# Hybrid diffusion step on one core: channel-mixer spills issued by GpSimd, modulation sums four steps behind, no modulation steps where the down product begins

## The chip, the cores and the metric

One core of a Trainium2 chip runs the whole step in one launch. The metric is the device time of that launch in microseconds. Engines are named as in the profile: PE (matrix products; PEld its weight loads), DVE (vector), ACT (scalar activations), POOL (GpSimd), SP (the queue that issues nearly all DMAs). All arithmetic is float32: a product of two float32 matrices is made of three matmuls, with each operand split into a rounded high part and the low rest.

## What is computed

Two layers over 1024 latent and 256 prompt tokens of width 1024. What matters here is the SwiGLU channel mixer that closes each layer, and the modulation vectors that scale, shift and gate every sub-layer:

```python
def swiglu(h, w_gate_up, w_down):
    gu = h @ w_gate_up
    return (jax.nn.silu(gu[..., :FFN_HIDDEN]) * gu[..., FFN_HIDDEN:]) @ w_down
for l in range(DEPTH):
    mod_p = jax.nn.silu(c_ctx) @ w_mod[l] + b_mod[l]
    mod_s = (jax.nn.silu(c) @ w_mod[l] + b_mod[l])[:, None, :]
    sh1_p, sc1_p, g1_p, sh2_p, sc2_p, g2_p = jnp.split(mod_p, 6, axis=-1)
    ...
    xp = xp + g2_p * swiglu(hp, w_gate_up[l], w_down[l])
    xs = xs + g2_s * swiglu(hs, w_gate_up[l], w_down[l])
```

`w_mod[l]` is 1024 x 6144, `w_gate_up[l]` 1024 x 5632, `w_down[l]` 2816 x 1024. In layer 0 a parallel mixer (windowed attention beside multi-scale pooling) comes before, in layer 1 grouped-query attention.

## The kernel before

Tokens stand in three tiles `ti`: 0 and 1 are 512 latent tokens each, 2 is the prompt's 256. The order on each engine is the order in which the code is written (`manual_schedule`), and an engine that waits holds back all that is written behind it on that engine. SP too is such a queue.

**The gate-up loop** (`ffn`, from L864). The hidden width is 22 chunks `i` of 128 (`NHC`). The two latent tiles are multiplied by a Strassen-like scheme: per chunk `front` (L913) and `back` (L999) make seven products of 12 matmuls each (`prod`, L879), named by their right operand Q11, Q21, T2, T1, T3, Q22, T4, and DVE, ACT and POOL add them up (in `back`, POOL does L1018 and L1019). The prompt tile has two plain products (`dense`, `prompt_gate` and `up_prompt`). Chunks 0 and 1 run interleaved in `begin` (L958); the others are the rounds 2 to 21. Each product fills one of eight PSUM buffers (`psd`), which is free again when DVE or ACT has read it.

**Weights.** Each round needs four weight units, G, A, B and U: G and U are halves of `w_gate_up` as loaded, A and B are sums of them. `Weights.make` (L261) builds A with L271 and L272, B with L274 and L275, on POOL from the 15th unit on; then ACT rounds the unit (L280) and DVE makes its low rest (L282). There are four unit buffers, and `W.done` makes the next unit as soon as one is used up, so a unit is built about a round before PE needs it. Raw weights come by SP (L251).

**Spills.** The finished hidden activations are split (`hi_lo`: ACT L767, DVE L768) into a staging tile and written to device memory: per round two of 512 KB through the one buffer `x2_1` (`spill`, L892, its DMA L900: first tile 1, from `c12`, then tile 0, from `c21`) and one of 256 KB (`up_prompt`, L938, its DMA L945). All three are issued by SP.

**Modulation.** While PE works on the gate-up loop, DVE makes the next modulation vectors (`Mod`, L357). A job is 512 columns: eight accumulate steps (two instructions each, L386 or L388, on one 256 KB tile that SP loads, L318, two tiles ahead), then two empty steps, then two sums (`sum`, L397: PE transposes the accumulator, L400, DVE reduces it, L401), then `mod_done`: 13 steps. `mstep` (L875) takes one step; it stands at six places of a round: after Q11 (here F1), after T2, T1, T3, Q22 and T4 (B1 to B5). Layer 0's mixer carries 12 jobs, layer 1's two. Other jobs run in the input projection of layer 0 (four) and its output projection (two).

**Down.** `down(q)` (L1038) multiplies six groups of chunks (`GROUPS`, 2 or 4 chunks) by `w_down`: 24 products per group (`mix`, L1058), each added to the residual by DVE (L1067). The activations come back by SP (`load_h`, L902) and so does the residual (`load_x`, L908). In groups 0 to 4 `mix` takes a modulation step after every product of tile 0.

Of the kernel before, what the change touches and what calls it, by code (L numbers as in the profile page):

```python
# [9 lines left out]
F32 = mybir.dt.float32  # L10
# [15 lines left out]
NHC = HID // 128  # L26
# [97 lines left out]
def hybrid_step(ctx: ExitStack, tc: tile.TileContext, I: dict, O: list):  # L124
    nc = tc.nc
    pe, act, dve, pool, sp = nc.tensor, nc.scalar, nc.vector, nc.gpsimd, nc.sync
# [65 lines left out]
    class Background:  # L192
# [12 lines left out]
        def step(self, n=1, now=1 << 30):  # L205
            for _ in range(n):
                if not self.q or self.q[0][1] > now or self.q.pop(0)[2]():
                    return
# [102 lines left out]
    def dense(ps, w, A, ti):  # L311
        for k in range(8):
            dense_k(ps, w, A, ti, k)
# [7 lines left out]
    def mod_done(l, j, v):  # L321

        o = modv[:, l, 4 * j:4 * j + 4, :]
        dve.tensor_tensor(o, v, bmod[:, l, 4 * j:4 * j + 4, None].to_broadcast([128, 4, 2]), op=OP.add)
        six, half = j // 2, j % 2
        if six in (1, 4):
            k = six // 4
            g = norms[:, 2 * l + k, 4 * half:4 * half + 4, None].to_broadcast([128, 4, 2])
            dve.scalar_tensor_tensor(moda[:, l, k, 4 * half:4 * half + 4, :], o, 1.0, g, op0=OP.add, op1=OP.mult)
# [27 lines left out]
    class Mod:  # L357
# [14 lines left out]
        def step(self):  # L372
            if self.pending:
                f = self.pending.pop(0)
                if f:
                    f()
                return True
            if self.pos >= len(self.tiles):
                return False
            l, j, k = self.tiles[self.pos]  # L380
            t = self.loaded.pop(self.pos)[:, 0]
            if k == 0:
                self.acc = [(self.sums or npool).tile([128, 512], F32, name="nacc", bufs=2) for _ in range(2)]
            for c, a in enumerate(self.acc):
                if k == 0:
                    dve.tensor_scalar(a, t, cond_raw[:, k, c:c + 1], 0.0, op0=OP.mult, op1=OP.add)  # L386
                else:
                    dve.scalar_tensor_tensor(a, t, cond_raw[:, k, c:c + 1], a, op0=OP.mult, op1=OP.add)  # L388
            self.pos += 1
            self.load(self.pos + self.bufs)  # L390
            if k == 7:
                acc, v = self.acc, npool.tile([128, 32], F32, name="mv", bufs=2)[:, 0:8].rearrange("p (b x) -> p b x", x=2)
                self.pending = [None, None, lambda: self.sum(acc[0], v, 0), lambda: self.sum(acc[1], v, 1),
                                lambda: mod_done(l, j, v)]
            return True

# [10 lines left out]
    def mvec(l, six, k, c):  # L407
        return modv[:, l, 8 * six + k, c:c + 1]
# [357 lines left out]
    def hi_lo(hi, lo, src):  # L766
        act.activation(hi, src, AF.Copy)  # L767
        dve.tensor_tensor(lo, src, hi.bitcast(F32), op=OP.subtract)  # L768
# [95 lines left out]
    def ffn(W, l, x, A, g2, tail, md, xr):  # L864
# [8 lines left out]
        H, now = {}, [0]  # L873

        def mstep():  # L875
            if md is not None and now[0] > 1:
                md.step()

        def prod(w, off, name):  # L879
            pt = ps_tile()  # L880
            t = quad[name]
            for c in range(4):
                wh, wl = w[:, 0, off + 128 * c:off + 128 * c + 128], w[:, 1, off + 128 * c:off + 128 * c + 128]
                pe.matmul(pt, wh, t(0, c), start=(c == 0), stop=False)  # L884
                pe.matmul(pt, wh, t(1, c), start=False, stop=False)  # L885
                pe.matmul(pt, wl, t(0, c), start=False, stop=(c == 3))  # L886
            return pt

        def place(i, ti):
            return hd[(i + 2) // 4][ti][:, :, i if i < 2 else (i + 2) % 4, :]  # L890

        def spill(i, ti, src):  # L892
            if i < NHC - 1:
                h = xp.tile([128, 2, 512], F32R, name="x2_1")
            elif ti == 0:
                h = gq.tile([128, 2, 512], F32R, name="wrawx")
            else:
                h = gq.tile([128, 2, 4, 512], F32R, name="T2")[:, :, 0]
            hi_lo(h[:, 0], h[:, 1], src)
            sp.dma_start(place(i, ti), h.bitcast(F32))  # L900

        def load_h(q, ti):  # L902
            t = slab(ti, q % 2) if ti == 2 else slab(q % 2, ti)
# [9 lines left out]
        def front(i, s):  # L913
            now[0] = i
            s["G"] = W.take(1)[0]
            w = s["G"][1]
            bg.need((0, 7))
            m = prod(w, 0, "Q11")
            a = s["a"] = gq.tile([128, 512], F32, name="ea", bufs=2)
            act.activation(a, m, AF.Copy)  # L920
            bg.step(5 if i else 3)
            mstep()
            m = prod(w, 512, "Q21")
            c = s["c"] = gq.tile([128, 512], F32, name="ec", bufs=2)
            dve.tensor_tensor(c, a, m, op=OP.add)
            act.activation(c, c, AF.Silu)
            bg.step(5)

        def prompt_gate(i, s):
            wi, w = s["G"]  # L930
            pg = ps_tile()
            dense(pg, w, A, 2)
            sg = s["sg"] = (npool.tile([128, 512], F32, name="nacc", bufs=2) if i < 2 else
                            npool.tile([128, 512], F32, name="s2", bufs=3))
            act.activation(sg[:, 0:256], pg[:, 0:256], AF.Silu)
            W.done(wi)
            bg.step(2)

        def up_prompt(i, s, w):
            pu, sg = ps_tile(), s["sg"]  # L940
            dense(pu, w, A, 2)
            dve.tensor_tensor(sg[:, 0:256], sg[:, 0:256], pu[:, 0:256], op=OP.mult)
            h = gq.tile([128, 2, 256], F32R, name="ph", bufs=1)
            hi_lo(h[:, 0], h[:, 1], sg[:, 0:256])
            sp.dma_start(place(i, 2), h.bitcast(F32))  # L945

        def c21(i, s, w, v):
            m = prod(w, 512, "T4")
            dve.tensor_tensor(v, v, m, op=OP.add)
            dve.tensor_tensor(s["c"], s["c"], v, op=OP.mult)  # L950
            spill(i, 0, s["c"])

        def c12(i, a, z):
            act.activation(a, a, AF.Silu)
            dve.tensor_tensor(a, a, z, op=OP.mult)
            spill(i, 1, a)

        def begin():  # L958

            for i in range(2):  # L960
                front(i, S[i])
                W.split(10 + i)
# [36 lines left out]
        def back(i, s):  # L999
# [3 lines left out]
            m = prod(w, 0, "T2")  # L1003
            dve.tensor_tensor(a, a, m, op=OP.add)
            mstep()
            m = prod(w, 512, "T1")
            z = npool.tile([128, 512], F32, name="s2", bufs=3)
            act.activation(z, m, AF.Copy)
            W.done(wi)
            mstep()  # L1010
            (wi, w), (ui, uw) = W.take(2 if last else 1) + ([] if last else [(None, None)])
            if last:
# [45 lines left out]
        def mix(q, m, ti, w, off, nm):  # L1058
            n, t, nk = TB[ti][1], H[q, ti], GROUPS[q]
            pt = ps_tile()  # L1060
            for k in range(nk):
                wh, wl = w[:, 0, off + 128 * k:off + 128 * k + 128], w[:, 1, off + 128 * k:off + 128 * k + 128]
                pe.matmul(pt[:, :n], wh, t[:, 0, k], start=(k == 0), stop=False)  # L1063
                pe.matmul(pt[:, :n], wh, t[:, 1, k], start=False, stop=False)  # L1064
                pe.matmul(pt[:, :n], wl, t[:, 0, k], start=False, stop=(k == nk - 1))  # L1065
            xc = x[ti][m]
            dve.scalar_tensor_tensor(xc, pt[:, :n], mvec(l, 5, m, COND[ti]), xc, op0=OP.mult, op1=OP.add)  # L1067
            if nm is not None:
                nm.feed(xc, pool if m < 6 else dve, sq)
            elif ti == 0:  # L1070
                mstep()

        NQ, sq = len(GROUPS), squares(gq)
# [2 lines left out]
        if md is not None:  # L1076
            md = Mod(Halves(wp.tile([128, 1024], F32, name="st")), md, 2)
        for i in range(2, NHC):
            front(i, S[i])
            if i == NHC - 1:  # L1080
                load_h(0, 0)
                load_h(0, 1)
                load_x(2)
            prompt_gate(i, S[i])
            back(i, S[i])
# [77 lines left out]
    md = Mod(st_pool, [(0, j) for j in range(4, 8)], 4)  # L1163
# [307 lines left out]
    md = Mod(mp, [(0, 8), (0, 9)], 3, mp)  # L1471
# [16 lines left out]
    md = [(0, 10), (0, 11)] + [(1, j) for j in range(10)]  # L1488
# [3 lines left out]
    def tail0(ti, nm):  # L1492
        for c in range(8):
            sp.dma_start(xs[ti][:, c, :], xt[ti][c])
        norm_tasks(nm, lambda c: xt[ti][c], 1, 0, ti, A1, ((4, 1), (7, 1), (0, 1))[ti])

    ffn(W, 0, xt, A, g2, tail0, md, xr)
    closers.pop()()

# [169 lines left out]
    def tail1(ti, nm):  # L1669
# [11 lines left out]
        for c in range(8):  # L1681
            bg.add((ti, 0), lambda c=c: f(c))

    ffn(W, 1, xt, A, g2, tail1, [(1, 10), (1, 11)], xr)
    bg.flush()
    closers.pop()()
# [35 lines left out]
```

## Time and profile before

| | |
|---|---|
| median of 3 runs | 3088.11 us (3081.44 to 3091.46) |
| the profiled execution | 3094.04 us, of which its span is 3092.3 us |
| PE busy | 2937.8 us (95%) |
| DVE busy | 1875.6 us (61%) |
| ACT busy | 1089.3 us (35%) |
| POOL busy | 822.8 us (27%) |
| share of the end's chain | PE 68%, DVE 11%, ACT 5%, POOL 3%, DMA 2% |

The layers' gate-up rounds 2 to 21 run from about 692 us to 1213 us (layer 0) and from about 2266 us to 2773 us (layer 1). In a timeline each line is one instruction, or several alike in a row (x2): start, duration, engine, source line, output and inputs, and in brackets how long the engine had been idle before it and what ended that. In a list of waits a line says who waited, for whom, how long in total, how many times and the longest.

### The profile page before, as it was taken

Reading aid. Unit: us, or ns where it says so; the run is one execution under the profiler, and the core shown is the slowest. Engines: PE = TensorE matmul, PEld = TensorE weight load, DVE = VectorE, ACT = ScalarE, POOL = GpSimd, SP = SyncE. Lnnn points to the kernel's source line nnn. Section 1 sums busy time; section 2 is a strip of 40 time slices with the busy share of each in tenths; the row PEclk is TensorE's granted clock in tenths of the full one; section 3 lists DMA queues with packets and bytes.
Section 4 is the critical chain, followed back from the end, with each engine's and each line's share of the span. In section 5 each row is a group of like instructions: output and inputs, shape, how many; then the busy total and the mean of one; then the engine's idle time right before and its main releaser. Section 6 shows DMA issues by size and latency. Waiting matters only on the chain.

```text
span 3092.3 us, 46174 instructions
## 1 busy us (share of the span) xinstructions
PE 2937.8 (95%) x18074; PEld 2489.7 (81%) x18074; DVE 1875.6 (61%) x3035; ACT 1089.3 (35%) x2084; POOL 822.8 (27%) x692
## 2 busy tenths in 40 slices
PE   6999999988999999899999999999789999999998
PEld 4878777867888887788878777878678888888887
DVE  5654665577777776544455688862767555554334
ACT  4233773343333332000332577761433333330002
POOL 0241542232333332000222344431323333320002
PEclk9999999989999999999999999999899999999999
DMA  6467644213434436543133410123033223255421
GB/s 248 146 194 228 154 128 154 89 49 129 136 127 130 133 126 237 203 172 138 68 122 141 154 59 31 36 83 99 24 130 116 92 93 101 102 180 204 177 102 69
DMA packets 184330, 394.55 MB, mean 128 GB/s; under 512 B 32176, under 2 KB 69424, under 8 KB 177840
## 3 DMA queue, kind: packets, MB, share of 16 engines
q1 hardware_dynamic: 180656, 385.34, 36.7%
q0 software_dynamic: 3456, 6.26, 0.8%
q8 instruction: 143, 2.34, 0.3%
q14 instruction: 75, 0.61, 0.1%
HBM read 274.32 MB, written 118.23 MB: 127 GB/s over the span
## 4 chain that ended last, share of the span: by engine, by line
PE 68%; DVE 11%; ACT 5%; issue 3%; POOL 3%; DMA 2%; SPq 0%; DVEq 0%; ACTq 0%; POOLq 0%
PE psd L1063 6%; PE psd L1065 6%; PE psd L1064 6%; PE psd L307 6%; PE psd L309 6%; PE psd L308 6%; PE psd L884 6%; PE psd L885 6%; PE psd L886 6%; PE ps_t L684 5%; PE ps_o L700 5%; PE ps_s L632 4%; DVE nacc L388 2%; ACT whl L280 2%; DVE whl L282 2%
## 5 line engine op out<-in xcount | busy, mean ns | idle before, releaser
L308 PE MATMUL psd<-A,whl 128*128 128x256 f32 (+1 forms) x1760 | 585.9, 333 | 16.0 <-DVE A L490 15.0
L307 PE MATMUL psd<-A,whl 128*128 128x256 f32 (+1 forms) x1760 | 588.9, 335 | 7.3 <-ACT A L454 2.7
L309 PE MATMUL psd<-A,whl 128*128 128x256 f32 (+1 forms) x1760 | 583.1, 331 | 2.0 <-DVE whl L282 2.0
L280 ACT ACTIVATE whl<-wraw 128x1024 fp32r<-128x1024 f32 x178 | 187.1, 1055 | 649.7 <-PE psd L1065 461.2
L1063 PE MATMUL psd<-A,whl 128*128 128x512 f32 (+1 forms) x1056 | 378.1, 358 | 16.3 <-DVE x L1067 10.3
L308 PEld LDWEIGHTS psd<-A,whl 128*128 128x128 f32 x1760 | 341.6, 194 | 52.5 <-DVE A L490 17.5
L1064 PE MATMUL psd<-A,whl 128*128 128x512 f32 (+1 forms) x1056 | 376.1, 356 | 0.0
L1065 PE MATMUL psd<-A,whl 128*128 128x512 f32 (+1 forms) x1056 | 376.0, 356 | 0.0
L307 PEld LDWEIGHTS psd<-A,whl 128*128 128x128 f32 x1760 | 342.2, 194 | 41.3 <-ACT A L454 3.2
L309 PEld LDWEIGHTS psd<-A,whl 128*128 128x128 f32 x1760 | 346.0, 197 | 31.7 <-DVE whl L282 3.3
L1067 DVE SCALAR_TENSOR_TENSOR x<-psd,modv,x 128x512 f32<-128x512 f32 (+1 forms) x288 | 186.9, 660 | 283.1 <-PE psd L1065 278.8
L282 DVE TENSOR_TENSOR whl<-wraw,whl 128x1024 fp32r<-128x1024 f32 x174 | 238.7, 1374 | 145.4 <-ACT whl L280 143.3
L884 PE MATMUL psd<-A,whl 128*128 128x512 f32 x704 | 277.4, 394 | 0.0
L885 PE MATMUL psd<-A,whl 128*128 128x512 f32 x704 | 275.4, 391 | 0.0
L886 PE MATMUL psd<-A,whl 128*128 128x512 f32 x704 | 275.4, 391 | 0.0
L674 POOL TENSOR_SCALAR sP<-sP,sm 128x896 f32<-128x896 f32 (+2 forms) x206 | 179.4, 875 | 245.8 <-DVE sm L667 120.0
L1063 PEld LDWEIGHTS psd<-A,whl 128*128 128x128 f32 x1056 | 201.1, 190 | 45.5 <-DVE x L1067 11.1
L1065 PEld LDWEIGHTS psd<-A,whl 128*128 128x128 f32 x1056 | 202.1, 191 | 28.0
L1064 PEld LDWEIGHTS psd<-A,whl 128*128 128x128 f32 x1056 | 201.1, 190 | 27.6
L684 PE MATMUL ps_t<-ident,sP 128*128 128x128 f32 x1408 | 206.6, 285 | 7.3 <-POOL sP L674 2.6
L426 POOL TENSOR_TENSOR nacc<-nacc,ec 128x512 f32<-128x512 f32 (+1 forms) x32 | 34.7, 1084 | 623.2 <-ACT ec L425 621.8
L684 PEld LDWEIGHTS ps_t<-ident,sP 128*128 128x128 f32 x1408 | 152.8, 143 | 57.3 <-issue 24.5
(224 smaller groups left out, 5246.6 us busy)
## 6 DMA issues: line engine op xcount, KB each, us to landing
hd<-x SPq DMA_DIRECT2D x84, 512.0 KB, 3.1
A<-hd SPq DMA_DIRECT2D x20, 2048.0 KB, 12.3
wraw<-in_w_gu_dram SPq DMA_DIRECT2D x60, 512.0 KB, 3.6
st<-in_w_mod_dram SPq DMA_DIRECT2D x112, 256.0 KB, 2.8
wraw<-in_w_down_dram SPq DMA_DIRECT2D x44, 512.0 KB, 3.7
wrawx<-in_w_gu_dram SPq DMA_DIRECT2D x28, 512.0 KB, 3.7
A<-hd SPq DMA_DIRECT2D x14, 1024.0 KB, 14.8
wmod<-in_w_mod_dram SPq DMA_DIRECT2D x48, 256.0 KB, 3.0
```

The costliest lines, as they stand in the source:

```text
L280: act.activation(h[:, 0], src, AF.Copy)
L282: eng.tensor_tensor(h[:, 1], src, h[:, 0].bitcast(F32), op=OP.subtract)
L307: pe.matmul(ps[:, :n], wh, A[ti].part(0, k), start=(k == 0), stop=False)
L308: pe.matmul(ps[:, :n], wh, A[ti].part(1, k), start=False, stop=False)
L309: pe.matmul(ps[:, :n], wl, A[ti].part(0, k), start=False, stop=(k == 7))
L684: pe.transpose(pt[:, 128 * (i - lo):128 * (i - lo) + 128], P[u][:, 128 * j:128 * j + 128], ident)
L884: pe.matmul(pt, wh, t(0, c), start=(c == 0), stop=False)
L885: pe.matmul(pt, wh, t(1, c), start=False, stop=False)
L886: pe.matmul(pt, wl, t(0, c), start=False, stop=(c == 3))
L1063: pe.matmul(pt[:, :n], wh, t[:, 0, k], start=(k == 0), stop=False)
L1064: pe.matmul(pt[:, :n], wh, t[:, 1, k], start=False, stop=False)
L1065: pe.matmul(pt[:, :n], wl, t[:, 0, k], start=False, stop=(k == nk - 1))
```

## The change

Three things. The spills of `spill` and `up_prompt` are issued by POOL instead of SP (66 DMAs per layer). A modulation job waits four empty steps instead of two between its last accumulate step and its sums, so it has 15 steps. And the places change: a seventh place F2 stands at the end of `front`, behind the product Q21; no step is taken in round 21 nor in group 0 of down; in groups 1 to 4 steps stand behind tile 0 and tile 2, two per row of the output instead of one.

```diff
-                self.pending = [None, None, lambda: self.sum(acc[0], v, 0), lambda: self.sum(acc[1], v, 1),
+                self.pending = [None, None, None, None, lambda: self.sum(acc[0], v, 0), lambda: self.sum(acc[1], v, 1),
...
         def mstep():
-            if md is not None and now[0] > 1:
+            if md is not None and 1 < now[0] < NHC - 1:
                 md.step()
...
             hi_lo(h[:, 0], h[:, 1], src)
-            sp.dma_start(place(i, ti), h.bitcast(F32))
+            pool.dma_start(place(i, ti), h.bitcast(F32))
...
             act.activation(c, c, AF.Silu)
             bg.step(5)
+            mstep()
...
             hi_lo(h[:, 0], h[:, 1], sg[:, 0:256])
-            sp.dma_start(place(i, 2), h.bitcast(F32))
+            pool.dma_start(place(i, 2), h.bitcast(F32))
...
             if nm is not None:
                 nm.feed(xc, pool if m < 6 else dve, sq)
-            elif ti == 0:
+            elif ti != 1 and q:
+                now[0] = 2
                 mstep()
```

Line numbers behind L927 are one higher in the changed kernel (two higher behind L1071).

How the order moves, at three places. POOL in one round of the loop (`s_6851` is the round's scratch tile; `x_0_6279` the scratch of A and B). Before:

```order
L1018 TENSOR_TENSOR ea<-ea,s_6851 128x512
L1019 TENSOR_TENSOR s_6851<-s_6871,s_6851 128x512
L274 TENSOR_TENSOR wrawx<-wrawx,wraw 128x512
L275 TENSOR_TENSOR wrawx<-wrawx,x_0_6279 128x512
L271 TENSOR_TENSOR x_0_6279<-wrawx 128x512
L272 TENSOR_TENSOR x_0_6279<-wraw,x_0_6279 128x512
```

and now:

```order
L1019 TENSOR_TENSOR ea<-ea,s_6851 128x512
L1020 TENSOR_TENSOR s_6851<-s_6871,s_6851 128x512
L900 DMA hd_1_1_6028<-x_1_6891 256x1x512
L274 TENSOR_TENSOR wrawx<-wrawx,wraw 128x512
L275 TENSOR_TENSOR wrawx<-wrawx,x_0_6279 128x512
L946 DMA hd_1_2_6029<-ph 256x1x256
L900 DMA hd_1_0_6027<-x_1_6953 256x1x512
L271 TENSOR_TENSOR x_0_6279<-wrawx 128x512
L272 TENSOR_TENSOR x_0_6279<-wraw,x_0_6279 128x512
```

The first spill now stands between L1020 and the two halves of unit B, the other two ahead of unit A.

POOL in `begin`, from the last norm instructions (L511) on. Before:

```order
L511 TENSOR_TENSOR x_7_6275<-s_6272,x_3_6274 128x512
L271 TENSOR_TENSOR x_0_6279<-wrawx 128x512
L272 TENSOR_TENSOR x_0_6279<-wraw,x_0_6279 128x512
L274 TENSOR_TENSOR wraw<-wraw,wrawx 128x512
L275 TENSOR_TENSOR wraw<-wraw,x_0_6279 128x512
L271 TENSOR_TENSOR x_0_6279<-wraw 128x512
```

and now:

```order
L511 TENSOR_TENSOR x_7_6275<-s_6272,x_3_6274 128x512
L900 DMA hd_0_1_6025<-x_1_6383 256x1x512
L946 DMA hd_0_2_6026<-ph 256x1x256
L900 DMA hd_0_0_6024<-x_1_6432 256x1x512
L271 TENSOR_TENSOR x_0_6279<-wrawx 128x512
L272 TENSOR_TENSOR x_0_6279<-wraw,x_0_6279 128x512
L274 TENSOR_TENSOR wraw<-wraw,wrawx 128x512
L275 TENSOR_TENSOR wraw<-wraw,x_0_6279 128x512
```

The units A and B of round 2 stand behind the three spills of chunk 0.

DVE at the beginning of round 2. Before:

```order
L386 TENSOR_SCALAR nacc<-st,cond_raw 128x512 x2
L925 TENSOR_TENSOR ec<-ea,psd 128x512
L282 TENSOR_TENSOR whl<-wraw,whl 128x1024
L1004 TENSOR_TENSOR ea<-ea,psd 128x512
L388 SCALAR_TENSOR_TENSOR nacc<-st,cond_raw,nacc 128x512 x2
L282 TENSOR_TENSOR whl<-x_0_6279,whl 128x1024
```

and now:

```order
L386 TENSOR_SCALAR nacc<-st,cond_raw 128x512 x2
L925 TENSOR_TENSOR ec<-ea,psd 128x512
L388 SCALAR_TENSOR_TENSOR nacc<-st,cond_raw,nacc 128x512 x2
L282 TENSOR_TENSOR whl<-wraw,whl 128x1024
L1005 TENSOR_TENSOR ea<-ea,psd 128x512
L388 SCALAR_TENSOR_TENSOR nacc<-st,cond_raw,nacc 128x512 x2
```

The step at F2 puts an accumulate pair between L925 and the low part of unit G.

## Rows read from the trace of the kernel before

**Rows 1.** Windows view, layer 0's rounds: length, then busy time of each engine (instructions).

```profile
711.40:1201.00 489.60, 475.31 (x2549) 412.09 (x2548) 378.65 (x454) 154.00 (x228) 169.97 (x112) 0.99 0.40 128
```

**Rows 2.** Waits of DVE, 711.4 to 1201 us: waiter, releaser, total, times, longest.

```profile
DVE whl L282 <- ACT whl L280: 47.9, 45, 1.9
...
DVE whl L282 <- DMA wraw<-in_w_gu_dram: 1.9, 1, 1.9
```

**Rows 3.** Waits of PE, 690 to 1270 us.

```profile
PE psd L400 <- DVE nacc L388: 14.3, 3, 8.1
PE psd L1063 <- DVE x L1067: 10.3, 2, 6.5
```

**Rows 4.** Timeline of DVE, end of tile 1's spill and unit B, round 14.

```profile
1010.68 1.01 DVE L768 TENSOR_TENSOR x<-ea,x 128x512 fp32r<-128x512 f32 x1 [0.70 <-ACT x L767]
1012.26 1.23 DVE L282 TENSOR_TENSOR whl<-wraw,whl 128x1024 fp32r<-128x1024 f32 x1 [0.58 <-ACT whl L280]
```

**Rows 5.** Timeline of POOL at the same place (unit B).

```profile
1008.15 1.28 POOL L274 TENSOR_TENSOR wraw<-wraw,wrawx 128x512 f32<-128x512 f32 x1
1009.39 1.74 POOL L275 TENSOR_TENSOR wraw<-wraw,x 128x512 f32<-128x512 f32 x1
```

**Rows 6.** Timeline of ACT at the same place.

```profile
1011.17 1.06 ACT L280 ACTIVATE whl<-wraw 128x1024 fp32r<-128x1024 f32 x1 [0.52 <-POOL wraw L275]
```

**Rows 7.** Source view of L1399, DMAs issued by POOL: min/median/max ns; then landing.

```profile
L1399 POOL DMA_DIRECT2D A<-yd x6: 742/752/828, 324.2 to 496.5; - x6
...
DMA to landing us min/median/max: 5.8/7.0/9.9
```

**Rows 8.** DVE groups, 711.4 to 1201 us: busy us, mean ns, idle before.

```profile
L955 DVE TENSOR_TENSOR ea<-ea,s 128x512 f32<-128x512 f32 x19 | 30.8, 1619 | 14.6 <-ACT ea L954 14.6
...
L768 DVE TENSOR_TENSOR x<-ec,x 128x512 fp32r<-128x512 f32 x19 | 20.0, 1051 | 14.2 <-ACT x L767 14.2
L768 DVE TENSOR_TENSOR x<-ea,x 128x512 fp32r<-128x512 f32 x19 | 19.0, 1002 | 13.3 <-ACT x L767 13.3
```

**Rows 9.** Timeline of DVE, round 21 into down, layer 0.

```profile
1201.07 0.68 DVE L925 TENSOR_TENSOR ec<-ea,psd 128x512 f32<-128x512 f32 x1
1203.66 1.23 DVE L282 TENSOR_TENSOR whl<-wraw,whl 128x1024 fp32r<-128x1024 f32 x1 [1.92 <-ACT whl L280]
...
1216.62 0.69 DVE L955 TENSOR_TENSOR ea<-ea,s 128x512 f32<-128x512 f32 x1 [0.69 <-ACT ea L954]
...
1220.09 1.41 DVE L388 SCALAR_TENSOR_TENSOR nacc<-st,cond_raw,nacc 128x512 f32<-128x512 f32 x2
...
1223.88 1.13 DVE L1067 SCALAR_TENSOR_TENSOR x<-psd,modv,x 128x256 f32<-128x256 f32 x2
...
1236.65 1.41 DVE L388 SCALAR_TENSOR_TENSOR nacc<-st,cond_raw,nacc 128x512 f32<-128x512 f32 x2 [7.80 <-DMA st<-in_w_mod_dram]
```

**Rows 10.** DVE in `begin`, layer 0: last spill of chunk 0, unit B.

```profile
690.86 0.69 DVE L768 TENSOR_TENSOR x<-ec,x 128x512 fp32r<-128x512 f32 x1 [1.14 <-ACT x L767]
...
692.95 1.22 DVE L282 TENSOR_TENSOR whl<-wraw,whl 128x1024 fp32r<-128x1024 f32 x1
```

**Rows 11.** Source view of L1063, group 0 of down, layer 0, then 1.

```profile
L1063 PE MATMUL psd<-A,whl x48: 276/389/792, 1219.6 to 1263.9; 128*128 128x512 f32 x32, 128*128 128x256 f32 x16
...
L1063 PE MATMUL psd<-A,whl x48: 279/389/392, 2774.3 to 2801.2; 128*128 128x512 f32 x32, 128*128 128x256 f32 x16
```

**Rows 12.** Timeline of PE: first product of group 1 of down, layer 0.

```profile
1264.93 0.48 PE L1063 MATMUL psd<-A,whl 128*128 128x512 f32 x1
```

**Rows 13.** Timeline of PE, round 3 of layer 1: the first transposes.

```profile
2319.48 1.11 PE L400 MATMUL psd<-ident,nacc 128*128 128x128 f32 x4 [9.93 <-DVE nacc L388]
```

**Rows 14.** Timeline of DVE, round 3 of layer 1.

```profile
2314.36 0.67 DVE L925 TENSOR_TENSOR ec<-ea,psd 128x512 f32<-128x512 f32 x1
```

**Rows 15.** Waits of PE, input projection, 140 to 275 us.

```profile
PE psd L400 <- DVE nacc L388: 3.3, 1, 3.3
```

**Rows 16.** DMA issues of the page: issuer, count, KB, us to landing.

```profile
hd<-x SPq DMA_DIRECT2D x84, 512.0 KB, 3.1
```

## Prediction

> **What bounds the kernel now.** PE is busy 95% of the span, so the first question is where it is not, and what it waits for there. The windows view of layer 0's rounds [rows 1] covers the 19 rounds from the DVE instruction L925 of round 2 to that of round 21: 489.6 us, 25.77 a round, of which PE is busy 475.31 (25.02 a round) and DVE only 378.65. PE's waits [rows 3] are few but telling: 14.3 us in three places, all at the transposes of a modulation job (L400), for the accumulator on DVE. So DVE lags behind PE and reins it in once per few jobs. DVE is at 77% and still late, because the rest of its time lies in hand-overs that stand in its order: its waits [rows 2] are 47.9 us in 45 places for ACT's rounding of a weight unit (at most 1.9 each), and only one wait is for a DMA. An engine that runs 19.9 us a round and hands over for some 5.8 is the bound at 25.8; every microsecond added to the DVE chain of a layer 0 round lengthens the round, but of what is removed only the first 0.75 us count (25.77 down to PE's 25.02).
>
> Layer 1 carries two jobs only, so its DVE has the time; PE waits 9.93 us at the first job's transposes in round 3 [rows 13], and DVE is then at the place shown in [rows 14].
>
> The third place is group 0 of down. In layer 0 it lasts from 1219.60 [rows 11] to 1264.93 [rows 12], 45.3 us; the same 48 long matmul groups in layer 1 need 2774.3 to 2801.8, 27.5 us [rows 11]. The cause stands in DVE's timeline [rows 9]: steps that wait up to 7.80 us for a modulation weight tile, with the additions L1067 behind them, so that PE runs out of PSUM buffers (10.3 us of waiting for L1067, [rows 3]).
>
> **The spills, in a round of layer 0.** SP issued them and lay on no one's way. Now POOL does, and POOL is an in-order engine that also builds the units A and B. The first spill must wait for DVE's L768, and the two halves of unit B (L274, L275) are written behind it. Before, they ran early: both were done before L768 ended [rows 4, 5], ACT rounded the unit beside it [rows 6], and DVE idled 0.58 us before L282 [rows 4]. Now the chain behind L768 is: hand-over 0.04, the issue 0.75 (median of POOL's DMAs, [rows 7]), L274 1.24 (start to start, [rows 5]), L275 1.28 (taken like its neighbour, as DVE idles then), hand-over 0.04, L280 1.06 [rows 6], hand-over 0.03: 4.44 us. DVE has nothing else written in between. That is +3.86 a round, and in 19 rounds **+73.3**.
>
> What is given back: L274 and L275 no longer run beside DVE's L955 and the L768 of tile 1. These take 1.62 and 1.00 us [rows 8], against 0.69 for an L955 beside an idle POOL [rows 9] and 0.69 for L768 [rows 10]: 19 x (0.93 + 0.31) = **-23.6**. The halves of unit A come behind the spill of tile 0 and leave its L768 alone (1.05 against 0.69, 6.9 in all), and fall on work of the next round: -6, bounds -6.9 and +6.9. The other two issues of a round, 0.75 each, may fall beside DVE's L282 of unit U. The trace has none there; the bounds are nothing and 0.67 x 19 = 12.7 (most of one issue each time), and I take the middle, **+6**.
>
> **The places, in the rounds.** A pair of accumulates takes 1.41 us [rows 9]. At F2 it falls behind L925, where DVE idles 1.92 us for ACT [rows 9]: in 11 of the 19 rounds F2 holds a pair, which is then free, **-15.5**. One round fewer hides its pair behind T3's product: **+1.5**. The two extra empty steps cost no instruction; they delay the transposes by two places, so PE's 14.3 us there can go. That is worth nothing in a stretch where DVE is the bound. Sum of the 19 rounds: 73.3 - 23.6 - 6 - 15.5 + 1.5 + 6 = **+35.7**, that is 27.65 us a round.
>
> **`begin`.** In the order of POOL the units A and B of round 2 now stand behind the three spills of chunk 0, the last of which needs L768 at 690.86 to 691.55 [rows 10]. Then an issue 0.75, L271 and L272, L274 and L275 (four times about 1.26) and L280 1.06, with hand-overs: about 699 for L282 of unit B, which ran at 692.95 [rows 10]: **+6.3** (5.8 to 6.8), at the start of the loop in either layer.
>
> **Round 21 and down.** L925 of round 21 moves from 1201.07 [rows 9] to 1201.07 + 6.3 + 35.7 = 1243.1. From it to the first product of group 1 there were 63.9 us [rows 9, 12]: 18.5 to down's first product, then 45.3. Now no step stands in either stretch: group 0 needs layer 1's 27.5, and the 18.5 shrink as far as DVE's lateness is caught up: between 10 (a lag of some 8 us gone) and 18.5; I take 14.5. So 42 (37.5 to 46), and group 1 begins at 1285.1, **+20.2**. Its 64 places have enough room: groups 1 to 4 run at PE's pace with steps in them today, and the pairs per product stay few.
>
> **Layer 1.** No detour shows there, since DVE has slack of several us a round with no steps. But up to round 3 its DVE is late by `begin`'s 6.3 and by the pair and unit that now come ahead of L925 (1.4 + 1.2): L925 at 2314.36 [rows 14] becomes 2323.3; PE, which went on at 2319.48 [rows 13], is then held by that, **+3.8** (2 to 6), and no longer by the transposes. **Input projection**: its four jobs wait 3.3 us at L400 [rows 15]; with two more empty steps that goes, **-3.3**. The output projection's two jobs have 32 places for 30 steps: nothing.
>
> **Sum**: 20.2 + 3.8 - 3.3 = +20.7. The profiled execution took 3094.04 us (span 3092.3), 5.9 above the median of 3088.11; against the median the forecast is **3109 us**.
>
> **Rivals.** *Faster* (0.25): the detour is smaller than I price it, because POOL's issue is not held up in its order, or is short. Speaking for it: all POOL DMAs of the trace are of another shape and place [rows 7]. Against: they are listed as POOL's own busy time. Then the rounds lose nothing: the F2 gain and the relief take DVE below PE, PE's 14.3 us of waits vanish [rows 3], `begin`'s 6.3 lie in the slack that this leaves DVE, and from L925 of round 21 to group 1 it is 63.9 - 42 = 21.9 shorter; layer 1 gains back half of its stall (-5), the input projection -3.3: -44, **3044**. The point that decides is the net detour per round: 20.7 us over 19 rounds, so below 3.86 - 1.1 = 2.75 us the change gains.
>
> *Landing* (0.12), slower still: SP's spills land 3.1 us after issue [rows 16], POOL's DMAs after 5.8 to 9.9 [rows 7]. Tile 0's `hi_lo` needs `x2_1` again, some 10 us after tile 1's spill. At 9.9 us ACT and DVE would wait in `begin`, where two spills share the buffer without a round between (twice 6.8 us, two layers, +27), and a little in the rounds: **3136**. Against: the median landing is 7.0 us.
>
> *DVE holds up the issue* (0.07). If POOL's issue can't proceed while DVE is at a long L282 (1.23 us, [rows 4]), each round loses up to this once more: 19 x 1.23 = +23, **3132**. The trace has no POOL DMA beside such an instruction: its issues range only from 742 to 828 ns [rows 7]. The Trainium skill ("SBUF — State Buffer", section "SBUF: two separate sides") has a rule that speaks against this change: a DMA issued by GpSimd has its descriptors written by GpSimd, which can't while DVE holds the port pair they share, so it waits for DVE. It names copies, not these subtractions of two tensors, and the page's example grows from about 620 to about 3100 ns; if it held for every first spill of a round, an estimate by that page would be 19 x 2.5 = 47 us more.
>
> *The change is worth nothing* (0.10): a detour of about 2.75 us, **3088**.
>
> **How the numbers follow.** My own case has 0.46, and with its bounds reaches from 3073 to 3136 (the A halves, the U issue, the 37.5 to 46, the detour itself by half a microsecond a round). What a measurement of this kernel can tell from no change is about 0.3%, 9 us: 3079 to 3097. Slower by more: 0.37 of my case, 0.12 and 0.07, 0.56; the same: 0.10 and 0.06 of my case, 0.16; faster: 0.25 and 0.03 of my low end, 0.28. The range takes in the faster rival and the landing one, 3044 to 3142.
>
> **What the profile after would show.** Right: DVE's gap before L282 behind the L768 of tile 1 is about 4.4 us in each round; POOL's L900 lasts about 0.75; L925 to L925 about 27.7 us; group 0 of layer 0 lasts about 27.5, with no wait for `st` and L1063 not waiting for DVE; no L400 waits in the input projection; layer 0's round 21 L925 near 1243. Wrong: rounds at 25 us with PE's waits gone (the faster rival); DVE or ACT waiting at L767 or L768 for a DMA (landing); POOL DMAs of 2 us and more (the port); or a wait that takes group 0's place in groups 1 to 4, where the steps now come twice per row.

## The result, and the profile after

The changed kernel takes 3138.65 us (median of 4 runs, 3137.11 to 3140.02) against 3089.4 for the kernel before in the runs beside it: a ratio of 1.0166, 95% interval 1.0152 to 1.0179. That is 49 us slower; forecast were 3109 us and 21 slower. The profiled executions differ by less, 3136.2 against 3092.3 us of span.

To find the 44 us, the trace is cut at the same instructions in every run: PE's first product of the gate-up loop, its first product of round 2, L925 of rounds 2 and 21 on DVE, the first product of down and the first of its groups 1 and 5. Start times of those instructions, subtracted:

| stretch, us | before | after | forecast change | change |
|---|---|---|---|---|
| launch to the gate-up loop of layer 0 | 620.0 | 614.5 | -3.3 | -5.5 |
| layer 0: first product of round 2 to its L925 | 18.8 | 26.3 | +6.3 | +7.5 |
| the 19 rounds, L925 to L925 | 489.75 | 532.9 | +35.7 | +43.1 |
| L925 of round 21 to down | 18.5 | 18.2 | -4.0 | -0.3 |
| group 0 of down | 45.3 | 30.1 | -17.8 | -15.2 |
| groups 1 to 4 | 221.8 | 222.6 | 0 | +0.8 |
| layer 1: round 2 to down | 508.8 | 520.9 | +3.8 | +12.1 |

The first line is not the change's. Eleven other kernels of this study and the changed one reach that place between 610.5 and 615.7 us; one of them has the same program as before up to there and needs 611.6. So the profiled execution of before was late there by itself, which fits its 5.9 us above its median. Without that line the stretches sum to +48, close to the 49 by which the medians differ.

**The rounds.** The windows view of the changed kernel over the same 19 rounds (length, then busy time of PE, PEld, DVE, ACT and POOL), against [rows 1]:

```profile
713.40:1246.20 532.80, 489.62 (x2520) 416.21 (x2521) 352.93 (x455) 153.73 (x228) 199.10 (x169) 0.96 0.37 118
```

DVE works 25.7 us *less* than before, in rounds that are 43.2 us longer. So its idle time grew by 69 us, and the list of its waits in that stretch says for what, against [rows 2] (no wait in the full list is for PE, now or before):

```profile
DVE whl L282 <- ACT whl L280: 110.3, 50, 5.9
...
DVE ea L956 <- ACT ea L955: 14.6, 19, 0.8
DVE ea L1028 <- POOL ea L1019: 11.7, 9, 1.5
...
DVE nacc L388 <- DMA st<-in_w_mod_dram: 5.6, 7, 0.9
```

PE's busy time grew too, by 14.3 us, at a mean granted clock of 0.96 against 0.99; as DVE never waits for PE here, that is not what makes these rounds longer.

The wait for ACT's L280 grew from 47.9 to 110.3 us. Where it sits, the timelines show: DVE around tile 1's spill in one round of layer 0, then POOL, then ACT at the same place, against [rows 4 to 6]:

```profile
1060.33 0.69 DVE L768 TENSOR_TENSOR x<-ea,x 128x512 fp32r<-128x512 f32 x1 [0.70 <-ACT x L767]
1065.69 1.23 DVE L282 TENSOR_TENSOR whl<-wraw,whl 128x1024 fp32r<-128x1024 f32 x1 [4.67 <-ACT whl L280]
```

```profile
1061.32 0.68 POOL L900 DMA_DIRECT2D hd<-x  x1 [2.50 <-DVE x L768]
1061.93 1.39 POOL L274 TENSOR_TENSOR wraw<-wraw 128x512 f32<-128x512 f32 x1
1063.18 1.39 POOL L275 TENSOR_TENSOR wraw<-wraw,x 128x512 f32<-128x512 f32 x1
```

```profile
1064.60 1.06 ACT L280 ACTIVATE whl<-wraw 128x1024 fp32r<-128x1024 f32 x1 [4.30 <-POOL wraw L275]
```

L768 ends at 1061.02; POOL issues the spill from 1061.32 on, and only then come L274 and L275, ACT's L280 at 1064.60, DVE's L282 at 1065.69. DVE idles 4.67 us where it idled 0.58 [rows 4]; over the 19 rounds this gap lies between 4.62 and 5.90 us. The issue itself is short: the source view of `spill`'s DMA over the whole run (duration min, median, max in ns; then us to landing), against [rows 7, 16]:

```profile
L900 POOL DMA_DIRECT2D hd<-x x84: 682/682/707, 681.6 to 2798.9; - x84
...
DMA to landing us min/median/max: 3.1/3.4/7.9
```

What DVE saved is in its groups (busy us, mean ns, idle before), the changed kernel first, against [rows 8]; for two groups that no row ahead shows, the lines of before follow:

```profile
L388 DVE SCALAR_TENSOR_TENSOR nacc<-st,cond_raw,nacc 128x512 f32<-128x512 f32 x126 | 115.9, 965 | 5.6 <-DMA st<-in_w_mod_dram 5.6
L282 DVE TENSOR_TENSOR whl<-wraw,whl 128x1024 fp32r<-128x1024 f32 x39 | 47.8, 1225 | 73.9 <-ACT whl L280 73.9
...
L768 DVE TENSOR_TENSOR x<-ec,x 128x512 fp32r<-128x512 f32 x19 | 13.2, 693 | 14.5 <-ACT x L767 14.5
L956 DVE TENSOR_TENSOR ea<-ea,s 128x512 f32<-128x512 f32 x19 | 13.2, 693 | 14.6 <-ACT ea L955 14.6
```

```profile
L388 DVE SCALAR_TENSOR_TENSOR nacc<-st,cond_raw,nacc 128x512 f32<-128x512 f32 x126 | 100.3, 841 | 0.0
L282 DVE TENSOR_TENSOR whl<-wraw,whl 128x1024 fp32r<-128x1024 f32 x39 | 59.7, 1532 | 33.5 <-ACT whl L280 31.5 <-DMA wraw<-in_w_gu_dram 1.9
```

L956 (L955 before) fell from 1.62 to 0.69 us, L768 of tile 0 from 1.05 to 0.69, L282 of `wraw` from 1.53 to 1.23, since POOL's halves no longer run beside them. The accumulates L388 rose from 0.84 to 0.97: unit A's halves run beside these now.

**Down.** PE's waits from round 2 to group 1 of down, against [rows 3], and the granted clock of PE (windows view, third number from the right, 0.50 being 1.2 GHz and 1.00 being 2.4; the next is the DMA share) before, at and after the first products of group 0:

```profile
PE psd L400 <- DVE nacc L388: 21.5, 6, 5.9
PE psd L1064 <- DMA A<-hd: 6.0, 1, 6.0
```

```profile
1252.40:1258.50 6.10, 6.10 (x27) 4.71 (x26) 2.47 (x6) 0.42 (x1) 3.30 (x3) 1.00 1.03 362
1264.40:1270.10 5.70, 5.64 (x16) 4.75 (x17) 2.96 (x4) 0.37 (x1) 0.18 (x1) 0.50 1.01 374
1270.10:1294.60 24.50, 24.50 (x130) 21.10 (x129) 14.26 (x22) 1.06 (x1) 0.00 (x0) 1.00 0.99 391
```

No wait for L1068 is left, and group 0 has lost 15 us. But PE still stands 6.0 us for the activations to come back (5.4 before), and the first 5.7 us behind that wait run at half clock. Before, they did so too: 0.50 from 1219.6 to 1225.0 us.

### The profile page after: what moved, and what is told of

It is laid out like the page before. It is cut to its first block, busy times and chain, and to the rows that moved or that the text cites. A ratio compares the mean times of both kernels' runs of the same rounds, so it can differ in the third digit from the quotient of the medians.

```text
span 3136.2 us, 46238 instructions
## 1 busy us (share of the span) xinstructions
PE 2956.4 (94%) x18074; PEld 2495.2 (80%) x18074; DVE 1819.0 (58%) x3035; ACT 1088.4 (35%) x2084; POOL 886.1 (28%) x824
## 4 chain that ended last, share of the span: by engine, by line
PE 65%; DVE 15%; ACT 7%; issue 6%; POOL 4%; DMA 4%; SPq 0%; DVEq 0%; ACTq 0%; POOLq 0%
PE psd L307 7%; PE psd L309 7%; PE psd L308 7%; PE psd L1064 6%; PE psd L1066 6%; PE psd L1065 6%; PE ps_t L684 5%; PE ps_o L700 5%; PE ps_s L632 4%; DVE nacc L388 4%; PE psd L884 4%; PE psd L886 4%; PE psd L885 4%; ACT whl L280 2%; DVE whl L282 1%
## 5 line engine op out<-in xcount | busy, mean ns | idle before, releaser
L280 ACT ACTIVATE whl<-wraw 128x1024 fp32r<-128x1024 f32 x178 | 187.1, 1055 | 743.4 <-PE psd L1066 447.7
L308 PEld LDWEIGHTS psd<-A,whl 128*128 128x128 f32 x1760 | 341.9, 194 | 53.4 <-DVE A L490 18.5
L282 DVE TENSOR_TENSOR whl<-wraw,whl 128x1024 fp32r<-128x1024 f32 x174 | 216.3, 1246 | 230.8 <-ACT whl L280 227.1
L1068 DVE SCALAR_TENSOR_TENSOR x<-psd,modv,x 128x512 f32<-128x512 f32 (+1 forms) x288 | 186.9, 660 | 273.9 <-PE psd L1066 269.4
L884 PE MATMUL psd<-A,whl 128*128 128x512 f32 x704 | 282.3, 401 | 14.9 <-DVE s L943 7.7
L886 PE MATMUL psd<-A,whl 128*128 128x512 f32 x704 | 280.5, 398 | 4.6 <-DVE whl L282 4.6
L885 PE MATMUL psd<-A,whl 128*128 128x512 f32 x704 | 279.3, 397 | 0.0
L684 PEld LDWEIGHTS ps_t<-ident,sP 128*128 128x128 f32 x1408 | 152.6, 143 | 56.1 <-issue 24.7
## 6 DMA issues: line engine op xcount, KB each, us to landing
hd<-x POOLq DMA_DIRECT2D x84, 512.0 KB, 3.3
A<-hd SPq DMA_DIRECT2D x20, 2048.0 KB, 12.1
wraw<-in_w_gu_dram SPq DMA_DIRECT2D x60, 512.0 KB, 3.7
wraw<-in_w_down_dram SPq DMA_DIRECT2D x44, 512.0 KB, 3.9
wrawx<-in_w_gu_dram SPq DMA_DIRECT2D x28, 512.0 KB, 3.7
```

The lines of the kernel that those rows point to most:

```text
L280: act.activation(h[:, 0], src, AF.Copy)
L282: eng.tensor_tensor(h[:, 1], src, h[:, 0].bitcast(F32), op=OP.subtract)
L308: pe.matmul(ps[:, :n], wh, A[ti].part(1, k), start=False, stop=False)
L684: pe.transpose(pt[:, 128 * (i - lo):128 * (i - lo) + 128], P[u][:, 128 * j:128 * j + 128], ident)
```

## The experiments

Stretches as in the table above, cut at the same instructions; the ratio is to runs of the kernel before on the same chip.

| kernel | early, layer 0 | 19 rounds | to down | group 0 | groups 1-4 | layer 1, round 2 to down | median us | ratio (95%) |
|---|---|---|---|---|---|---|---|---|
| before | 18.8 | 489.75 | 18.5 | 45.3 | 221.8 | 508.8 | 3089.4 | 1 |
| changed | 26.3 | 532.9 | 18.2 | 30.1 | 222.6 | 520.9 | 3138.65 | 1.0166 (1.0152-1.0179) |
| spills alone | 26.0 | 547.2 | 18.5 | 44.8 | 221.8 | 522.3 | 3169.64 | 1.0277 (1.0262-1.0293) |
| places and lag alone | 19.0 | 482.5 | 19.4 | 29.8 | 222.6 | 502.0 | 3059.98 | 0.9919 (0.9904-0.9934) |
| tile 1 on SP | 25.5 | 478.9 | 18.1 | 29.3 | 222.6 | 508.7 | 3069.01 | 0.9950 (0.9934-0.9967) |
| issue behind unit B | 26.4 | 482.1 | 19.1 | 29.6 | 222.6 | 509.4 | 3072.55 | 0.9957 (0.9942-0.9972) |
| `begin` on SP | 18.7 | 534.1 | 17.8 | 29.1 | 222.7 | 514.7 | 3124.67 | 1.0119 (1.0103-1.0135) |
| `begin` and tile 1 on SP | 18.7 | 478.7 | 18.2 | 29.5 | 222.6 | 504.0 | 3056.87 | 0.9894 (0.9879-0.9908) |
| lag alone | 18.8 | 476.7 | 19.7 | 42.2 | 241.4 | 499.0 | 3086.75 | 0.9993 (0.9983-1.0003) |
| four issues | 26.3 | 546.5 | 18.9 | 30.2 | 222.6 | 525.7 | 3158.25 | 1.0221 (1.0206-1.0236) |
| only tile 1 on POOL | 18.8 | 534.1 | 18.7 | 30.0 | 222.6 | 513.6 | 3125.05 | 1.0116 (1.0100-1.0131) |
| places alone, lag two | 18.7 | 496.0 | 18.2 | 29.1 | 221.2 | 512.0 | 3085.73 | 0.9992 (0.9981-1.0002) |
| tile 1 on SP, layer 1, rounds 2-6 | 26.2 | 532.75 | 18.2 | 30.4 | 222.7 | 512.6 | 3128.73 | 1.0126 (1.0109-1.0143) |

**The two halves of the change.** Spills alone is the kernel before with

```diff
-            sp.dma_start(place(i, ti), h.bitcast(F32))
+            pool.dma_start(place(i, ti), h.bitcast(F32))
...
-            sp.dma_start(place(i, 2), h.bitcast(F32))
+            pool.dma_start(place(i, 2), h.bitcast(F32))
```

> The kernel before with the spills on POOL, nothing else. Theory (order: POOL's spill of tile 1 stands ahead of unit B's halves, so that DVE, the bound of layer 0's rounds, waits 4.67 us for unit B behind it instead of 0.58): layer 0's 19 rounds gain 19 x 4.09 = 78 us of waiting and lose about 26 of contention, without the 15.5 that F2 gives back: some 60 to 70 us slower in all (3145 to 3165). Rival (the new places or the longer lag cost the time): at most 15 us slower.

and places and lag alone is the changed kernel with these lines undone.

> The changed kernel with the spills back on SP: the places and the lag alone. Theory: layer 0's rounds go at PE's pace (about 14 us less), the stretch from L925 of round 21 to group 1 is 15 to 20 us shorter, the input projection 5, layer 1's first rounds up to 5: 3040 to 3055. Rival (places or lag cost the time): 3085 or more.

Measured: 84 us slower, and 25 faster. The theory holds in both signs. The 19 rounds of spills alone grew by 57.4 us, near the 78 of waiting less 26 of relief; the total is 5 us beyond its upper bound, and layer 1, which the expectation left out, lost 13.5. It was too hopeful on places and lag: 3060, not 3055 or less, the rounds 7 us shorter and not 14. DVE's waits in those rounds point to why:

```profile
DVE whl L282 <- ACT whl L280: 30.1, 40, 1.9
...
DVE nacc L388 <- DMA st<-in_w_mod_dram: 10.7, 9, 2.0
```

The wait for ACT fell by 17.8 us, near the 15.5 forecast for F2, and a new one took 10.7 of it: the pairs at F1, F2 and B1 stand close together, and the modulation tiles, which SP loads two ahead, come too late for them (a reading of the order, not tried by itself).

**What of the spills costs.** Two ways to take the wait away: tile 1's spill alone goes back to SP,

```diff
-            pool.dma_start(place(i, ti), h.bitcast(F32))
+            (pool if ti == 0 else sp).dma_start(place(i, ti), h.bitcast(F32))
```

> The changed kernel with only tile 1's spill back on SP; POOL still issues the prompt's and tile 0's. Theory (what counts is what stands behind the issue on POOL): the 4.67 us wait is gone and the time is near that of places and lag alone, 3040 to 3065. Rival (an issue by POOL costs by itself, by its landing or by what it does to DVE): two thirds of the loss stay, 3100 or more.

or POOL keeps all three and only the order of two things is swapped in `back`:

```diff
-            c12(i, a, z)
+            go = c12(i, a, z, True)
             W.done(wi)
+            go()
```

with `spill` returning its DMA instead of issuing it when told so.

> The changed kernel with POOL issuing all spills, but in the rounds tile 1's is written behind the two halves of unit B instead of ahead of them. Theory: the same as with tile 1 on SP, 3040 to 3065, since the wait behind L768 is gone though POOL issues as many DMAs. Rival (issue by POOL by itself): no change, 3130 to 3140.

Both fell to 3069 and 3073, a little beyond the bounds of theory (3065) but some 65 us or more under the changed kernel, and the rounds to 478.9 and 482.1. The second is the clean one: it issues as many DMAs on the same engine, in the same rounds, and one of them stands two instructions later. Its POOL and DVE in one round of layer 0:

```profile
1026.00 1.27 POOL L274 TENSOR_TENSOR wraw<-wraw 128x512 f32<-128x512 f32 x1
1027.24 1.74 POOL L275 TENSOR_TENSOR wraw<-wraw,x 128x512 f32<-128x512 f32 x1
1029.83 0.68 POOL L900 DMA_DIRECT2D hd<-x  x1 [0.85 <-DVE x L768]
```

```profile
1026.15 1.67 DVE L959 TENSOR_TENSOR ea<-ea,s 128x512 f32<-128x512 f32 x1 [0.77 <-ACT ea L958]
1028.53 1.00 DVE L768 TENSOR_TENSOR x<-ea,x 128x512 fp32r<-128x512 f32 x1 [0.70 <-ACT x L767]
1030.10 1.23 DVE L282 TENSOR_TENSOR whl<-wraw,whl 128x1024 fp32r<-128x1024 f32 x1 [0.57 <-ACT whl L280]
```

L274 runs while DVE is at L959 (1.67 us again, against 0.69), and L282 waits 0.57. What both keep is the late beginning, 25.5 and 26.4 us instead of 18.8, because in `begin` POOL still issues tile 0's spill, the last of the three, ahead of units A and B. Layer 1 also stays some 7 us above places and lag alone. That is what was missing to 3060.

**One issue out of three, and the beginning.**

```diff
-            pool.dma_start(place(i, ti), h.bitcast(F32))
+            (pool if ti == 1 and i > 1 else sp).dma_start(place(i, ti), h.bitcast(F32))
...
-            pool.dma_start(place(i, 2), h.bitcast(F32))
+            sp.dma_start(place(i, 2), h.bitcast(F32))
```

> The changed kernel with only tile 1's spills of rounds 2 to 21 on POOL; begin's, the prompt's and tile 0's are back on SP. Theory (one issue per round carries the loss): the 19 rounds of layer 0 stay at 528 to 540 us, the early stretch is back at 19, total 3120 to 3135. Rival (the three issues of a round share the loss): the rounds at about 500 us, 3080 to 3095.

The 19 rounds took 534.1 us, no less than the changed kernel's 532.9. One DMA of three carries the loss in the rounds. The other two, prompt and tile 0, cost nothing there, taken together with the halves of unit A, which move with tile 0's spill.

```diff
-            pool.dma_start(place(i, ti), h.bitcast(F32))
+            (sp if i < 2 else pool).dma_start(place(i, ti), h.bitcast(F32))
...
-            pool.dma_start(place(i, 2), h.bitcast(F32))
+            (sp if i < 2 else pool).dma_start(place(i, 2), h.bitcast(F32))
```

> The changed kernel with the spills of begin (chunks 0 and 1) back on SP, those of the rounds on POOL. Theory: the stretch from round 2 to its L925, 26.3 us in the changed kernel, falls to about 19 in both layers, and nothing else changes in layer 0; in layer 1, whose DVE has modulation steps only until round 6, begin's 7.5 us are part of the 12 lost, so that about half stays: 3122 to 3128 in all. Rival (layer 1's loss is not begin's, PE waits in rounds 2 to 6 for the detour alone): layer 1 keeps its 12 and the total falls by 7, to about 3131.

The early stretch is back at 18.7, the total 14 lower and layer 1 6.2 lower, as theory said. In the changed kernel's `begin` DVE waits twice, for A and for B, since POOL builds them only behind the third spill:

```profile
686.48 0.69 POOL L900 DMA_DIRECT2D hd<-x  x1 [2.98 <-DVE x L768]
687.07 1.42 POOL L271 TENSOR_TENSOR x<-wrawx 128x512 f32<-128x512 f32 x1
...
691.20 2.27 POOL L275 TENSOR_TENSOR wraw<-wraw,x 128x512 f32<-128x512 f32 x1
```

```profile
685.50 0.69 DVE L768 TENSOR_TENSOR x<-ec,x 128x512 fp32r<-128x512 f32 x1 [1.67 <-ACT x L767]
690.99 1.33 DVE L282 TENSOR_TENSOR whl<-x,whl 128x1024 fp32r<-128x1024 f32 x1 [4.80 <-ACT whl L280]
694.60 1.23 DVE L282 TENSOR_TENSOR whl<-wraw,whl 128x1024 fp32r<-128x1024 f32 x1 [2.27 <-ACT whl L280]
```

That is the case of [rows 10], with L282 of unit B now 9.1 us behind the start of L768 where it was 2.1.

**A dose.** Tile 1's spill in four quarters, each a DMA of its own:

```diff
-            pool.dma_start(place(i, ti), h.bitcast(F32))
+            if ti == 1 and 1 < i < NHC - 1:
+                for r in range(2):
+                    for p in range(2):
+                        pool.dma_start(place(i, ti)[64 * p:64 * p + 64, r], h[64 * p:64 * p + 64, r].bitcast(F32))
+            else:
+                pool.dma_start(place(i, ti), h.bitcast(F32))
```

> The changed kernel with tile 1's spill of each round of 2 to 20 issued by POOL as four DMAs of a quarter each, the same bytes. Theory (what stands ahead of unit B's halves on POOL is paid one for one in layer 0's rounds): three more issues of some 0.6 us, 1.8 us a round, 19 rounds, +35; layer 1's first four rounds +7: 3175 to 3190. Rival (landing or the memory's traffic sets the time, the issue does not): within 5 us of 3138.

Slower by 20 us, not by 36 or more. The expectation took four issues in a row behind L768. But two of them carry the rounded half, which ACT writes, and needn't wait for L768; POOL's row shows the four begin with ACT as releaser, and DVE's that the wait is 5.37 us, 0.70 over the changed kernel's:

```profile
1064.84 2.12 POOL L903 DMA_DIRECT2D hd<-x  x4 [1.77 <-ACT x L767]
1066.97 1.29 POOL L274 TENSOR_TENSOR wraw<-wraw 128x512 f32<-128x512 f32 x1
```

```profile
1064.58 0.69 DVE L768 TENSOR_TENSOR x<-ea,x 128x512 fp32r<-128x512 f32 x1 [0.70 <-ACT x L767]
1070.64 1.23 DVE L282 TENSOR_TENSOR whl<-wraw,whl 128x1024 fp32r<-128x1024 f32 x1 [5.37 <-ACT whl L280]
```

19 x 0.70 = 13.3, and the 19 rounds grew by 13.6. So the dose was mis-sized, and what reached the chain was paid one for one. The rival, a time within 5 us of 3138, is out.

**Layer 1.** Tile 1 on SP in five rounds of layer 1:

```diff
-            pool.dma_start(place(i, ti), h.bitcast(F32))
+            (sp if l == 1 and ti == 1 and 1 < i < 7 else pool).dma_start(place(i, ti), h.bitcast(F32))
```

> The changed kernel with tile 1's spill on SP in rounds 2 to 6 of layer 1 only. Theory (layer 1 pays for the wait only while it has modulation steps, rounds 2 to 6): its stretch from round 2 to down falls from 520.9 to about 509, as with tile 1 on SP everywhere (508.7); total 3126 to 3130. Rival (every round of layer 1 pays a little, or begin's lateness carries it): less than 5 us of the 12 come back, 3134 or more.

The stretch fell from 520.9 to 512.6, 8.3 of the 12 back (509 was expected), and the total to 3128.7, as expected. In rounds 7 to 21 POOL still issues tile 1's spill ahead of unit B; that costs layer 1 at most the few microseconds left. In the changed kernel the gap before L282 is 4.7 us in every round of layer 1, but only the rounds with steps pay: from L925 to L925 the first four take 112.0 us (112.1 in layer 0), and from round 9 on each takes 24.7. PE's waits in layer 1's first rounds show what the wait costs there; before there was only that of [rows 13]:

```profile
PE psd L400 <- DVE nacc L388: 6.7, 2, 5.5
PE psd L884 <- ACT whl L280: 3.2, 2, 2.9
PE psd L884 <- DVE s L943: 2.2, 1, 2.2
```

**Lag and places apart.**

```diff
-                self.pending = [None, None, lambda: self.sum(acc[0], v, 0), lambda: self.sum(acc[1], v, 1),
+                self.pending = [None, None, None, None, lambda: self.sum(acc[0], v, 0), lambda: self.sum(acc[1], v, 1),
```

> The kernel before with four empty steps instead of two, nothing else. Theory (layer 0's rounds are bound by DVE's chain, so PE's waits at the transposes are only where its lead is given back): the 14.3 us of waits at L400 shrink or move to other products and the 19 rounds stay within 4 us of 489.8; layer 1 up to 5 less; 3080 to 3090. Rival (the waits at the transposes are what costs): 14 us less in layer 0, 3065 to 3075.

In the kernel before this is no change in time (0.9993), as theory said, but neither theory had it right inside. The 19 rounds got 13.0 us shorter, as the rival said, and layer 1 9.8, about its wait of [rows 13]. And groups 1 to 4 got 19.6 longer: of 180 steps only 160 have a place, and the rest run in one piece at the end, where PE waits 17.5 us for them:

```profile
702.50:1179.30 476.80, 472.65 (x2545) 408.41 (x2543) 366.87 (x436) 153.64 (x228) 167.46 (x112) 1.00 0.39 127
```

```profile
L388 DVE SCALAR_TENSOR_TENSOR nacc<-st,cond_raw,nacc x112: 735/744/1781, 706.9 to 1173.1; 128x512 f32<-128x512 f32 x112
```

```profile
PE psd L400 <- DVE nacc L388: 17.5, 1, 17.5
```

In the rounds DVE's busy time fell by 12 (366.87 against 378.65), with 112 accumulates instead of 126: jobs of 15 steps on the same places put fewer of them in. So the gain can be the thinner DVE chain as well as the waits at L400 that are gone; this run does not tell the two apart.

The opposite, the new places with the old lag (the changed kernel with spills on SP and two empty steps):

> The new places alone: spills on SP and two empty steps as before. Jobs of 13 steps on the new places mean 10.2 jobs in the 19 rounds instead of 8.9. Theory (the rounds are DVE's chain, and the empty steps thin it): some 10 more pairs of 1.41 us, 14 us more than places and lag together, the 19 rounds at 490 to 500, and later waits at the transposes as large as before; total 3060 to 3075, as the steps end earlier. Rival (the lag is without effect beside the places): 482 us, 3055 to 3063.

The rounds came out as expected, 496.0 us, with 18.7 us of PE's waits at L400, and the total did not: 3085.73, since layer 1 too took 10 us more than with places and lag together. Either half alone gives nothing that can be measured here; together they give 25 us.

**The better version.** From this follows POOL for tile 0 and the prompt in the rounds alone:

```diff
-            pool.dma_start(place(i, ti), h.bitcast(F32))
+            (sp if i < 2 or ti == 1 else pool).dma_start(place(i, ti), h.bitcast(F32))
...
-            pool.dma_start(place(i, 2), h.bitcast(F32))
+            (sp if i < 2 else pool).dma_start(place(i, 2), h.bitcast(F32))
```

> The changed kernel with begin's spills and tile 1's on SP; POOL issues only the prompt's and tile 0's in the rounds, which puts unit A's halves behind tile 0's spill. Theory: the early stretch as with places and lag alone (19 us), the 19 rounds as with tile 1 alone on SP (478.9 us against 482.5), so at or a little under places and lag alone: 3050 to 3062. Rival (what the delayed unit A gave in the rounds was taken from elsewhere): 3065 or more.

3056.87 us, 0.9894 (0.9879 to 0.9908): 1.1% under the kernel before and 2.6% under the changed one. Its interval overlaps that of places and lag alone by a little (0.9904 to 0.9908), so that the further gain is likely, not shown.

## Why the prediction was right in its direction and wrong in its size

The direction came out, and +49 us where +21 were forecast. Without the input projection the terms of the forecast sum to +24.0, the measured stretches to +48.0. Of the 24.0 that were missing, 8.3 lie in layer 1, 7.4 in layer 0's rounds, 6.3 on the way into down and its group 0, 1.2 in `begin` and 0.8 in groups 1 to 4.

**Right: the mechanism and its place.** The forecast had the spill of tile 1 ahead of unit B on POOL, DVE as the bound of layer 0's rounds, and a gap of 4.4 us before L282; the gap is 4.67, with 0.30 us from L768 to the issue where 0.04 were taken. One DMA swapped with two instructions takes 51 us out of the rounds, so this is shown. In the rounds the terms stand thus: the detour 19 x (4.67 - 0.58) = 77.7 (forecast 73.3); the relief of L956 and of tile 1's L768 -23.4 (-23.6); the rest of the change in the waits for L280, put down to F2, -15.3 (-15.5); L1028 +2.7 (+1.5).

**Right by luck: unit A's halves.** L768 of tile 0 -6.8 and L282 -17.3 of busy time, L388 and L386 +19.4: -4.7 (forecast -6). The forecast priced neither the relief on L282 nor what fell on the accumulates; they nearly cancel.

**Wrong, small: the two other issues.** +6 was taken for POOL's issues beside L282 of unit U. They cost nothing: L282 takes 1.22 to 1.23 us at the mean of each unit. Two costs that the forecast did not price made up for it: 5.6 us for modulation tiles that F2 uses up early (1.9 for raw weights went), and 2.2 more for the eight L324 (0.48 us each for 0.21). Together the rounds are 7.4 over their forecast.

**Wrong: layer 1.** "No detour shows there, since DVE has slack of several us a round with no steps." Layer 1 has its 30 steps in rounds 2 to 6, and the first four of those take as long as layer 0's (112.0 and 112.1 us); the forecast took the pace of the rounds without steps for all. Against places and lag alone, where this stretch takes 502.0, the changed kernel loses 18.9 us: 6.2 come back with `begin` on SP, 8.3 with tile 1 on SP in rounds 2 to 6, each alone; the last 4.4 are not separated. The step took 3.8 where 12.1 was measured; it is the largest miss of the sum.

**Wrong: the way into down.** The forecast let "the 18.5 shrink as far as DVE's lateness is caught up". They don't, in any of the twelve kernels (17.8 to 19.7), because loads set them and not DVE. SP issues the first load of activations within 0.5 us of L925; the one that the first product reads is issued some 12 us later, behind eight residual loads, and lands 6.2 us after that:

```profile
1246.17 1.23 SPq L905 DMA_DIRECT2D A<-hd  x2
1247.45 9.54 SPq L911 DMA_DIRECT2D x<-xr  x8
...
1258.08 0.52 SPq L905 DMA_DIRECT2D A<-hd  x1
```

In all thirteen kernels that product starts 0.13 to 0.14 us after this landing, and the DMA share around it is 1.0 in the windows above. PE waits 6.0 us for it here and 5.4 before. That wait stood in the list of PE's waits of before and was not used:

```profile
PE psd L1063 <- DMA A<-hd: 5.4, 1, 5.4
```

And group 0 was given layer 1's 27.5 us; behind the wait PE runs 5.7 us at half clock, of which half, 2.8, is lost by an estimate from the two clocks, and group 0 took 30.1. Together +6.3.

**Rivals.** Faster: the detour was to decide at 2.75 us a round, and it is 4.09; with the wait gone the time was 3060 (3069 and 3073 where `begin` stayed late) and not 3044: in places and lag alone the rounds are some 7 us above that rival's sum, and the way into down with group 0 another 7. Landing: 3.4 us at the median, not 5.8 to 9.9, and ACT waits for a spill's landing 11.1 us in four places, 11.9 before; it is out. DVE holds up the issue: 84 issues took 682 to 707 ns, one of them at 1071.51 us beside an L282 that began at 1071.47. Of all 132 spill issues 42 lie wholly beside an L282, and none of those takes more than 692 ns, so it is out too. The Trainium skill's rule behind that rival ("SBUF — State Buffer", section "SBUF: two separate sides") names operations in a two-port fast mode, float32 copies among them, and this trace doesn't contradict it: no copy runs beside these issues, and the subtraction of two tensors does not bring the stall.

The sum was also set against a profiled execution whose excess lay ahead of the gate-up loop; the -3.3 for the input projection can't be told from the scatter there. PE's 3.3 us at L400 did go, as forecast, but its other waits from 140 to 275 us grew from 1.8 to 6.8, so PE's waiting moved there and did not go.

## What to carry to other kernels

A DMA moved to another engine takes that engine's order with it: what must be asked is not how long the issue lasts (0.68 us here) but what the issue waits for, and what is written behind it. Writing two instructions ahead of it was worth as much as moving it back. Before a stretch is given another's pace, its waits that remain must be listed: here loads and the half-clock products behind them kept 6 us, and layer 1's first rounds were bound like layer 0's because they carry the same steps.

## What the runs showed of the hardware that was not expected

POOL's issue of 512 KB lasted 0.68 us, as that of 256 KB did, and that of a quarter of 512 KB 0.53 to 0.57; landing came 3.4 us after, against 3.1 by SP [rows 16]. The 5.8 to 9.9 us of the six DMAs in [rows 7] were no guide to it.

How much DVE and POOL slow each other depends on the instructions: in the changed kernel L386, which reads one tile and a column, takes 0.48 us alone and up to 1.52 beside POOL's halves, an accumulate L388 0.74 to 0.75 alone and up to 1.79. POOL's L275 takes 1.36 to 1.40 alone and 1.74 beside DVE [rows 5]. A relief at one place was paid back at the next: -24.1 us and +19.4 for the two halves of unit A.
